# A scheduler's clock for the tensor engine: charging the change between dense and tiled products

## The chip, the core and the metric

The kernel runs on one core of a Trainium2 chip. TensorE (PE) multiplies, VectorE (DVE), ScalarE (ACT) and GpSimd (POOL) work element by element, SyncE (SP) issues DMAs. Each engine takes its own instructions strictly in the order in which they were written, and waits at a semaphore where an operand is not there yet. The metric is the device time of one execution in microseconds (us), median of several runs. Before the change it was 2242.0 us (three runs, 2240.91 to 2247.69).

## The reference

Two transformer blocks over 512 tokens of width 1024, all in float32. The first block (one layer) has three mixers side by side: dilated attention, a gated linear attention (GLA) and block attention. The second block (two layers, with a second stream of 256 context tokens in the first of them) has a Fourier mixer, grouped attention and a gated recurrence (HGRN). Each layer ends in a feed-forward part. The part that matters here is the decay inside GLA and HGRN:

```
# GLA                                           # HGRN, both directions
log_a = log_sigmoid(a_lr @ w_a2 + b_a) / 16     cum   = cumsum(lf, axis=2)
diff  = b[..., :, None, :] - b[..., None, :, :]  diff  = cum[:, :, :, None, :] - cum[:, :, None, :, :]
decay = exp(where(causal, diff, -inf))          decay = exp(where(mask, diff, -inf))
attn  = einsum('ic,jc,ijc->ij', q, k, decay)    att   = einsum('td,sd,tsd->ts', q, k, decay)
```

The rest is matrix products with large weights: `proj = h @ w_in`, `x + mix @ w_out`, `square(relu(h2 @ w_ff1)) @ w_ff2`, `(silu(h @ wg) * (h @ wu)) @ wd`, and the modulation vectors `silu_c @ w_ada`.

## The kernel before, in words

**Dense products.** Every weight tile (128x1024) comes by DMA into a `raw` buffer, is rounded by ACT (`hi`) and its remainder is taken by DVE (`lo`) in the task `split`. A product of a weight block with an activation block then takes three matmuls (hi by hi, hi by lo, lo by hi) into a PSUM tile named `psm` or `psx`. One such triple, 512 or 256 columns wide, is one operation for the scheduler.

**Tiled products.** The decay is not formed pair by pair. GLA and HGRN work in levels of 1, 2, 4, 8 and 16 positions (`LOW`, then 32 and 64). At each level `low_gram` (line 1074) forms small products of 32 columns, placed in different tiles of the PE array, into a PSUM tile named `psd`; DVE copies what the level's mask selects (`copy_predicated`, line 1092). Then `decay_step` or `bidir_level` (lines 1048 and 2046) multiplies K and Q by that level's decay, on DVE or on POOL, whichever the scheduler finds earlier, and `bidir_gram` (line 2061) copies K into order for the next level. So each level of a segment waits for elementwise work of the level before. One `low_gram` is one PE operation of 16 small products (32 in GLA). There are 84 such groups: 14 in GLA (first block), 14 in HGRN over the context, 28 in HGRN of the second block's layer 0 (tasks `hg00`, `hg01`, `hg10`, `hg11`), 28 in layer 1. Below these are stages 1 to 4: a stage runs from the first such group to the last.

**Who sets the order.** The whole kernel is written as Python generators (tasks) that yield operations. `Sched.run` (line 565) keeps a clock for each engine and a finish time for each buffer, asks which pending operation could start earliest by these clocks, writes that one and advances its engine's clock by the operation's `cost`. It runs while the program is built; on the chip only the resulting order of each engine is left. Where an operation may go to several engines (`alt`), the same clocks choose. The table of costs is the planner's, for instance, for a group of tiled products and for a 256-column triple:

```
base = 4 * n / 2.4
if m <= 32:
    return max(32, base / 4 + 14)          # 32 ns each: 512 ns for 16, 1024 ns for 32
...
op.thin = cost < 40 * len(mms)             # in PE(): true for these groups alone
```

A 256-column triple is put down at 333 ns, a 512-column triple at 646 ns. `THIN = (0.7, 500.0, 1.0)` is a second rule for these groups: `s.thin` grows by a group's cost and falls by 0.7 of every other PE cost; above 500 the next group is put back by that much. `s.port` keeps a POOL operation and a DVE operation with two SBUF inputs apart on the planner's clocks.

Of the kernel before, what the change touches and what calls it, by code (L numbers as in the profile page):

```python
# [229 lines left out]
class Fut:  # L230
# [4 lines left out]
    def __init__(s, v=None):  # L235
        s.v, s.ok = v, v is not None
# [199 lines left out]
class Sched:  # L436
# [6 lines left out]
    def __init__(s, tc, pools, counts):  # L443
        s.tc, s.nc = tc, tc.nc
        nc = s.nc
        s.eng = {"pe": nc.tensor, "act": nc.scalar, "dve": nc.vector, "pool": nc.gpsimd, "sp": nc.sync}
        s.clock = {e: 0.0 for e in s.eng}
        s.busy = {e: 0.0 for e in s.eng}
        s.wr, s.rd, s.wre = {}, {}, {}
        s.pools = pools  # L450
        s.freel = {k: list(range(c)) for k, c in counts.items()}
        s.avail = {}
        s.owner = {}
        s.who = {}
        s.tasks = []
        s.n = 0
        s.table = None
        s.thin = 0.0
        s.hold = 0.0
        s.port = {"dve": 0.0, "pool": 0.0}  # L460
        s.low = {k: c for k, c in counts.items()}
        s.marks = []
# [75 lines left out]
    def emit(s, op, st, who=''):  # L538
        e = op.eng
        eng = s.eng[e]  # L540
        if op.table is not None and op.table != s.table:
            eng.preload_act_table_set(SETS[op.table])
        for fn, a, k in op.calls:
            r = getattr(eng, fn)(*a, **k)  # L544
            if s.log is not None:
                s.log.append((r, e, fn, st, op, who))
        cost = op.cost
        if op.table is not None and op.table != s.table:
            cost += 1300
            s.table = op.table  # L550
        end = st + cost
        if e == "pe":
            s.thin = s.thin + cost if op.thin else max(0.0, s.thin - THIN[0] * cost)
        s.clock[e] = end
        if op.port:
            s.port[e] = end
        s.busy[e] += cost
        fin = end + op.lat
        for n in op.outs:
            s.wr[n] = max(s.wr.get(n, 0.0), fin)  # L560
            s.wre[n] = e
        for n in op.ins:
            s.rd[n] = max(s.rd.get(n, 0.0), end if e == "pe" else end + 40)
# [2210 lines left out]
```

## Time and profile before

| | |
|---|---|
| median of 3 runs | 2242.0 us |
| profiled execution | 2240.0 us, of which the span of the trace is 2238.2 us |
| PE busy | 2210.3 us (99% of the span) |
| weight loads of PE | 1924.0 us (86%) |
| DVE busy | 1560.7 us (70%) |
| ACT busy | 916.4 us (41%) |
| POOL busy | 112.7 us (5%) |
| granted TensorE clock | 0.999 of full speed |

A busy PE means that matmul records follow each other without a hole; matmuls overlap, so the length of a record is more than its share of the time. What a product costs is read from the distance between starts. An idle PE is a hole in that chain, and there are 27.9 us of it.

### The profile page before, as it was taken

How to read it: one execution, taken by the hardware profiler on the slowest of the kernel's cores; microseconds unless marked ns; L12 is line 12 of the kernel's file. 1: busy time of each engine (PE TensorE's matmuls, PEld its weight loads, DVE VectorE, ACT ScalarE, POOL GpSimd, SP SyncE). 2: the span in 40 equal slices, each digit the busy share in tenths (PEclk: the TensorE clock that was granted, in tenths of full speed). 3: DMA queues.
4: the chain of work that ended last, by engine and by line, in shares of the span. 5: the costliest groups of instructions: out<-in, count | busy, mean ns of one | idle time of the engine just before them, and what ended most of it. 6: DMA issues, size and time to landing. Idle time of an engine off the chain costs nothing.

```text
span 2238.2 us, 42398 instructions
## 1 busy us (share of the span) xinstructions
PE 2210.3 (99%) x17071; PEld 1924.0 (86%) x17071; DVE 1560.7 (70%) x3754; ACT 916.4 (41%) x1679; POOL 112.7 (5%) x118
## 2 busy tenths in 40 slices
PE   9999999999999999999999999999999999999998
PEld 7887988788888879899888888889979899888887
DVE  6888976888888898798765443557787876444446
ACT  5465644452224455764212112124545754222224
POOL 0100002000000030000000000000040000000000
PEclk9999999999999999999999999999999999999999
DMA  5446443334444621343333212433321223222223
GB/s 197 139 146 189 176 149 125 137 128 146 146 155 166 216 78 48 104 143 138 144 126 128 95 66 78 136 136 119 113 66 58 77 86 123 94 95 102 96 94 113
DMA packets 92116, 272.69 MB, mean 122 GB/s; under 512 B 10944, under 2 KB 20952, under 8 KB 91920
## 3 DMA queue, kind: packets, MB, share of 16 engines
q1 hardware_dynamic: 91920, 269.99, 35.8%
q8 instruction: 134, 2.20, 0.4%
q14 instruction: 62, 0.51, 0.1%
HBM read 253.66 MB, written 7.38 MB: 117 GB/s over the span
## 4 chain that ended last, share of the span: by engine, by line
PE 91%; DVE 4%; DMA 2%; ACT 2%; issue 1%; SPq 0%; DVEq 0%; ACTq 0%
PE psm L544 69%; PE psx L544 18%; PE psd L544 4%; DVE slot L544 3%; DMA rawc<-wada 1%; DVE wu L544 1%; ACT wu L544 1%; ACT slot L544 1%; DMA slot<-ctx 0%; SPq L544 0%; DMA slot<-x 0%; DMA slot<-slot 0%; DMA rawc<-w2in 0%; ACT pr L544 0%; DVE sm L544 0%
## 5 line engine op out<-in xcount | busy, mean ns | idle before, releaser
L544 PE MATMUL psm<-slot,wu 128*128 128x512 f32 (+1 forms) x8406 | 1542.8, 341 | 6.6 <-DVE slot L544 5.0
L544 PEld LDWEIGHTS psm<-slot,wu 128*128 128x128 f32 x8406 | 1305.6, 190 | 188.1 <-DVE slot L544 8.1
L544 ACT CAST wu<-raw 128x1024 fp32r<-128x1024 f32 (+1 forms) x325 | 340.5, 1048 | 860.0 <-PE psm L544 479.1
L544 DVE TENSOR_TENSOR wu<-raw,wu 128x1024 fp32r<-128x1024 f32 (+1 forms) x325 | 402.3, 1238 | 180.8 <-ACT wu L544 175.5
L544 DVE CUSTOM_DVE_ANT_0 slot<-rawc,slot 128x256 f32<-128x256 f32 x640 | 271.4, 424 | 100.7 <-DMA rawc<-wada 90.5
L544 DVE TENSOR_TENSOR slot<-slot,slot 128x256 f32<-128x256 f32 (+5 forms) x362 | 197.0, 554 | 15.2 <-ACT slot L544 12.5
L544 PE MATMUL psm<-wu,slot 128*128 128x256 f32 x1296 | 181.5, 289 | 0.0
L544 DVE SCALAR_TENSOR_TENSOR slot<-psm,mods,slot 128x256 f32<-128x256 f32 (+1 forms) x190 | 108.5, 572 | 104.4 <-PE psm L544 103.2
L544 DVE TENSOR_TENSOR slot<-slot,psm 128x512 f32<-128x512 f32 (+1 forms) x202 | 118.6, 594 | 76.4 <-PE psm L544 71.5
L544 PEld LDWEIGHTS psm<-wu,slot 128*128 128x128 f32 x1296 | 162.7, 191 | 4.0 <-issue 1.2
L544 PE MATMUL psx<-slot,wu 128*128 128x512 f32 (+1 forms) x858 | 164.1, 346 | 0.1
L544 PEld LDWEIGHTS psx<-slot,wu 128*128 128x128 f32 x858 | 137.1, 190 | 19.2 <-DVE wu L544 0.3
L544 PE MATMUL psd<-slot,slot 64*32 64x32 f32 (+6 forms) x3616 | 124.5, 216 | 6.0 <-issue 2.5
L544 PEld LDWEIGHTS psd<-slot,slot 64*32 64x32 f32 (+4 forms) x3616 | 93.5, 116 | 35.7 <-issue 15.8
L544 PE MATMUL psx<-slot,slot 128*64 128x128 f32 (+5 forms) x1554 | 121.3, 281 | 0.9 <-ACT slot L544 0.7
L544 POOL TENSOR_TENSOR slot<-slot,slot 128x256 f32<-128x256 f32 (+1 forms) x72 | 72.6, 1016 | 951.9 <-DVE slot L544 820.1
L544 ACT CAST slot<-slot 128x512 fp32r<-128x512 f32 (+3 forms) x142 | 79.7, 561 | 77.0 <-DVE slot L544 73.9
L544 PEld LDWEIGHTS psx<-slot,slot 128*64 128x64 f32 (+3 forms) x1554 | 91.1, 139 | 23.3 <-issue 10.9
L544 ACT COPY slot<-psx 128x256 f32<-128x256 f32 (+5 forms) x191 | 78.2, 421 | 61.5 <-PE psx L544 53.0
L544 ACT ACTIVATE slot<-slot 128x256 f32<-128x256 f32 (+1 forms) x150 | 65.3, 456 | 33.3 <-DVE slot L544 28.5
L544 ACT ACTIVATE pr<-psd,sm 128x768 f32<-128x768 f32 (+1 forms) x80 | 65.1, 816 | 19.8 <-DVE sm L544 19.1
L544 DVE SCALAR_TENSOR_TENSOR slot<-slot,mods,slot 128x256 fp32r<-128x256 f32 (+2 forms) x152 | 69.0, 492 | 4.6 <-ACT slot L544 4.5
(100 smaller groups left out, 1334.4 us busy)
## 6 DMA issues: line engine op xcount, KB each, us to landing
rawc<-wada SPq DMA_DIRECT2D x96, 512.0 KB, 4.5
raw<-w2gu SPq DMA_DIRECT2D x88, 512.0 KB, 3.3
raw<-w1ff SPq DMA_DIRECT2D x64, 512.0 KB, 3.3
raw<-w2da SPq DMA_DIRECT2D x56, 512.0 KB, 3.2
raw<-w2in SPq DMA_DIRECT2D x36, 512.0 KB, 3.4
raw<-w2out SPq DMA_DIRECT2D x24, 512.0 KB, 3.7
raw<-w1in SPq DMA_DIRECT2D x23, 512.0 KB, 4.0
rawc<-w2in SPq DMA_DIRECT2D x18, 512.0 KB, 3.3
```

What stands on the lines that cost most here:

```text
L544: r = getattr(eng, fn)(*a, **k)
```

## The change

The scheduler remembers whether the last PE operation was a tiled group. When the next one is of the other kind, PE's clock advances by 89 more (dense to tiled) or 210 more (tiled back to anything else). Nothing else is edited: no instruction is added or removed by hand, no buffer and no cost table.

```
@@ -456,6 +456,7 @@
         s.table = None
         s.thin = 0.0
+        s.was_thin = False
         s.hold = 0.0
@@ -548,6 +549,9 @@
         if op.table is not None and op.table != s.table:
             cost += 1300
             s.table = op.table
+        if e == "pe" and op.thin != s.was_thin:
+            cost += 89 if op.thin else 210
+            s.was_thin = op.thin
         end = st + cost
         if e == "pe":
             s.thin = s.thin + cost if op.thin else max(0.0, s.thin - THIN[0] * cost)
```

What comes of it is another order. Both programs have the same 4271 PE operations and the same 84 tiled groups, each of them alone between other work, so 84 changes there and 84 back in either. The first rows below are PE's in stage 4, from one tiled group of a segment on (`psd` is the tiled groups' PSUM tile, `psm` the dense products'; `32x32 x16` is one group, and a row `128x256 x3` one triple). Before:

```order
L544 MATMUL psd_3167_17610<-slot_3161_17533,slot_3166_17608 32x32 x16
L544 MATMUL psm_3169_17614<-wu_3135_17411,slot_2952_16322 128x256 x3
L544 MATMUL psm_3169_17614<-wu_3135_17411,slot_2953_16332 128x256 x3
L544 MATMUL psm_3169_17614<-wu_3135_17411,slot_2955_16343 128x256 x3
L544 MATMUL psd_3178_17649<-slot_3158_17527,slot_3177_17639 32x32 x16
L544 MATMUL psm_3169_17614<-wu_3135_17411,slot_2960_16364 128x256 x3
L544 MATMUL psm_3169_17614<-wu_3135_17411,slot_2952_16322 128x256 x3
L544 MATMUL psm_3169_17614<-wu_3135_17411,slot_2953_16332 128x256 x3
L544 MATMUL psm_3169_17614<-wu_3135_17411,slot_2955_16343 128x256 x3
L544 MATMUL psm_3169_17614<-wu_3135_17411,slot_2960_16364 128x256 x3
L544 MATMUL psm_3169_17614<-wu_3147_17463,slot_2963_16378 128x256 x3
L544 MATMUL psd_3181_17698<-slot_3158_17527,slot_3180_17696 32x32 x16
```

And PE's rows at the same place now, from the same group on:

```order
L545 MATMUL psd_3167_17591<-slot_3161_17533,slot_3166_17589 32x32 x16
L545 MATMUL psm_3146_17462<-slot_3058_16828,wu_3126_17338 128x512
L545 MATMUL psm_3146_17462<-slot_3059_16829,wu_3126_17338 128x512
L545 MATMUL psm_3146_17462<-slot_3058_16828,wu_3126_17338 128x512
L545 MATMUL psd_3168_17616<-slot_3158_17524,slot_3166_17589 32x32 x16
L545 MATMUL psm_3170_17636<-wu_3135_17411,slot_2952_16322 128x256 x3
L545 MATMUL psd_3174_17645<-slot_3161_17533,slot_3173_17643 32x32 x16
L545 MATMUL psm_3170_17636<-wu_3135_17411,slot_2953_16332 128x256 x3
L545 MATMUL psd_3181_17672<-slot_3172_17638,slot_3173_17643 32x32 x16
```

Three triples and then six stood between the groups; now it is one each time, and the triples that stood here come later. Over whole stages, rows of PE's order from the first tiled group to the last: 151 and 114 (stage 1), 144 and 110, 165 and 145, 155 and 100 (stage 4).

The second place is POOL in stage 4, the multiplies of K (`slot_3087`, `slot_3088`) and Q (`slot_3158`) by the decay of the segments `hg00` and `hg01`. Before:

```order
L544 TENSOR_TENSOR slot_3087_17034<-slot_3087_17034,slot_3159_17529 128x32x2x4
L544 TENSOR_TENSOR slot_3087_17034<-slot_3087_17034,slot_3159_17529 128x16x2x8
L544 TENSOR_TENSOR slot_3158_17527<-slot_3158_17527,slot_3159_17529 128x16x2x8
L544 TENSOR_TENSOR slot_3087_17034<-slot_3087_17034,slot_3159_17529 128x8x2x16
L544 TENSOR_TENSOR slot_3088_17035<-slot_3088_17035,slot_3162_17538 128x16x2x8
L544 TENSOR_TENSOR slot_3088_17035<-slot_3088_17035,slot_3162_17538 128x8x2x16
```

And now, from the same multiply on:

```order
L545 TENSOR_TENSOR slot_3087_17034<-slot_3087_17034,slot_3159_17526 128x32x2x4
L545 TENSOR_TENSOR slot_3088_17035<-slot_3088_17035,slot_3162_17535 128x32x2x4
L545 TENSOR_TENSOR slot_3087_17034<-slot_3087_17034,slot_3159_17526 128x16x2x8
L545 TENSOR_TENSOR slot_3088_17035<-slot_3088_17035,slot_3162_17535 128x16x2x8
L545 TENSOR_TENSOR slot_3087_17034<-slot_3087_17034,slot_3159_17526 128x8x2x16
L545 TENSOR_TENSOR slot_3158_17524<-slot_3158_17524,slot_3159_17526 128x8x2x16
L545 TENSOR_TENSOR slot_3098_17109<-slot_3098_17109,slot_3096_17107 128x128x2
L545 TENSOR_TENSOR slot_3184_17720<-slot_3184_17720,slot_3096_17107 128x128x2
L545 TENSOR_TENSOR slot_3087_17034<-slot_3087_17034,slot_3159_17526 128x4x2x32
L545 TENSOR_TENSOR slot_3158_17524<-slot_3158_17524,slot_3159_17526 128x4x2x32
```

More of the multiplies have gone to POOL here: 28 within stage 4, where there were 21. On DVE, operations between the masked copy of a stage's first group and that of its last are 84 before and 72 now in stage 1, 85 and 81 in stage 2, 124 and 127 in stage 3, 121 and 105 in stage 4. POOL's are 11 and 8, 15 and 12, 20 and 21, 21 and 28.

The dense triples within the stages, counted the same way on PE: 256 columns wide 31 and 20, 24 and 24, 55 and 46, 58 and 32; 512 columns wide 16 and 16, 33 and 23, 6 and 6, 6 and 6. Of other small PE operations (transposes, 64-column products, attention) 8, 2, 2 and 3 fewer stand within the stages now.

## Rows read from the trace of the kernel before

**Rows 1.** The page: span, and busy us by engine.
```profile
span 2238.2 us, 42398 instructions
PE 2210.3 (99%) x17071; PEld 1924.0 (86%) x17071; DVE 1560.7 (70%) x3754; ACT 916.4 (41%) x1679; POOL 112.7 (5%) x118
```

**Rows 2.** Stretches: stages 1 to 4, then two of attention; length, then busy us.
```profile
core 0: us, PE busy (x) PEld busy (x) DVE busy (x) ACT busy (x) POOL busy (x), PEclk, DMA share, GB/s
39.75:79.95 40.20, 38.89 (x1008) 32.24 (x1011) 34.40 (x120) 13.80 (x32) 6.29 (x9) 1.00 0.43 130
364.70:406.70 42.00, 41.30 (x657) 32.04 (x662) 39.69 (x95) 19.06 (x33) 16.54 (x15) 1.00 0.33 108
787.50:832.60 45.10, 43.16 (x1160) 35.63 (x1161) 44.15 (x128) 22.75 (x57) 18.95 (x20) 1.00 0.23 66
1633.00:1680.00 47.00, 44.07 (x1186) 36.63 (x1183) 42.54 (x122) 21.42 (x56) 20.77 (x21) 1.00 0.18 57
850.00:900.00 50.00, 49.85 (x428) 44.81 (x427) 42.79 (x90) 32.98 (x78) 2.96 (x2) 1.00 0.14 43
1700.00:1750.00 50.00, 50.00 (x426) 45.75 (x425) 40.28 (x82) 30.64 (x75) 5.65 (x4) 1.00 0.14 43
```

**Rows 3.** Timeline of PE in dense stretches: start us, length us, operation, count.
```profile
1030.75 3.04 PE L544 MATMUL psx<-slot,wu 128*128 128x256 f32 x24
1033.63 5.92 PE L544 MATMUL psm<-slot,wu 128*128 128x256 f32 x48
...
1206.18 5.63 PE L544 MATMUL psx<-slot,wu 128*128 128x512 f32 x24
1211.65 0.62 PE L544 MATMUL psm<-slot,wu 128*128 128x512 f32 x2
```

**Rows 4.** Timeline near the end of stage 4 (a group of 16 shows as x32).
```profile
1669.90 0.41 DVE L544 TENSOR_TENSOR slot<-slot,slot 128x256 f32<-128x256 f32 x1
1669.92 0.89 POOL L544 TENSOR_TENSOR slot<-slot,slot 128x256 f32<-128x256 f32 x1 [0.53 <-ACT slot L544]
...
1669.93 0.35 PE L544 MATMUL psd<-slot,slot 64*32 64x32 f32 x32
...
1670.22 0.97 PE L544 MATMUL psx<-wu,slot 128*128 128x256 f32 x6
1670.23 0.66 DVE L544 TENSOR_TENSOR slot<-slot 128x64 f32<-128x64 f32 x1
1670.82 0.29 DVE L544 COPY_PREDICATED slot<-c_masks,psd 128x128 f32<-128x128 int32 x1
...
1671.11 0.35 PE L544 MATMUL psd<-slot,slot 64*32 64x32 f32 x32
```

**Rows 5.** Timeline in the middle of stage 4, up to a wait of PE.
```profile
1654.46 1.93 POOL L544 TENSOR_TENSOR slot<-slot,slot 128x256 f32<-128x256 f32 x2 [5.34 <-DVE slot L544]
...
1655.32 1.22 DVE L544 COPY slot<-slot 128x64 f32<-128x64 f32 x2
...
1657.51 0.79 PE L544 MATMUL psd<-slot,slot 64*64 64x64 f32 x48 [1.12 <-DVE slot L544]
...
1660.35 0.60 PE L544 MATMUL psx<-c_ident,slot 128*128 128x128 f32 x4
```

**Rows 6.** Groups on POOL by form: count, busy us, mean ns, idle before.
```profile
L544 POOL TENSOR_TENSOR slot<-slot,slot 128x256 f32<-128x256 f32 x63 | 59.9, 961 | 803.1 <-DVE slot L544 718.8 <-PE psd L544 77.3 <-DVE part L544 5.7
L544 POOL TENSOR_TENSOR slot<-slot,sm 128x256 f32<-128x256 f32 x3 | 1.8, 611 | 0.8 <-DVE sm L544 0.8
```

**Rows 7.** Who PE waited for over the whole span: us, times, longest.
```profile
PE psm L544 <- DVE slot L544: 5.0, 12, 1.4
PE psx L544 <- DVE slot L544: 4.9, 7, 1.8
...
PE psd L544 <- DVE slot L544: 2.1, 4, 1.1
```

More of the change, by code (lines that the diff above doesn't have):

```diff
@@ L458, in __init__ @@
         s.thin = 0.0
+        s.was_thin = False
         s.hold = 0.0
@@ L550, in emit @@
             s.table = op.table
+        if e == "pe" and op.thin != s.was_thin:
+            cost += 89 if op.thin else 210
+            s.was_thin = op.thin
         end = st + cost
```

## The prediction

> **What bounds the kernel now.** I read the page first: PE is busy for 2210.3 of 2238.2 us and no other engine for more than 70% [rows 1]. So the time is PE's work plus 27.9 us of holes, and no order can take away the work. Then I looked at who ends PE's holes: it is mostly DVE (5.0, 4.9 and 2.1 us for its three kinds of PSUM tile) [rows 7]. The share of 70% is a mean over unlike stretches, so the third view was the busy time by stretch, cut at the four stages in which the tiled groups stand. There DVE is busy for 34.40 of 40.20, 39.69 of 42.00, 44.15 of 45.10 and 42.54 of 47.00 us, PE for 38.89, 41.30, 43.16 and 44.07 [rows 2]. In stage 3 DVE has less room left (0.95 us) than PE (1.94 us). These 174.30 us are the place where the change acts, and in them two engines run side by side at nearly full load. PE's idle time there is 1.31 + 0.70 + 1.94 + 2.93 = 6.9 us.
>
> **What is charged, and what it takes.** A row of 24 products of 256 columns starts at 1030.75 and the next row at 1033.63, so one product has 0.120 us and a triple 0.36; with 512 columns it is (1211.65 - 1206.18) / 24 = 0.228, a triple 0.684 [rows 3]. The planner has 0.333 and 0.646: too little. Now a tiled group: it starts at 1669.93, the dense row behind it at 1670.22, and the next group at 1671.11 [rows 4]. The group itself takes 0.29, and the six dense products have 0.89 where 0.72 would do, so the change there and back costs 0.17. Group and both changes take 0.46 us. The planner had put down 0.512 for the group alone, which covered them already; now it puts down 0.512 + 0.089 + 0.210 = 0.81. It was 0.05 us too dear and is 0.35 us too dear. (In GLA's groups of 32 the base is 1.024.)
>
> [...]
>
> **The change part by part.** No instruction goes or comes, so PE's work as a whole stays: 0 us. The number of changes stays: 0 us. What moves is which dense triples stand within the stages. While elementwise work readies the next tiled group, the planner fills PE; each group now uses up 0.3 us more of that wait on PE's clock, so fewer triples fit. The second rule on these groups is not what moves them: before, one 256-column triple brought its account from 512 to 279, below the 500 at which it acts; now from 601 to 221.
>
> Between the first and the last group of each stage there is less PE work, then, while the elementwise work of 84 levels is still all there. I price both sides for each stage. A 256-column triple counts 0.36, a 512-column one 0.684, one of the small operations 0.6 (four transposes had 0.60 [rows 5]). DVE's demand I take as its busy time, scaled by the operations in its order, since records and waits for POOL are all in that time.
>
> Stage 1: 11 triples of 0.36 and 8 small operations leave, 4.0 + 4.8; PE has 38.89 - 8.8 = 30.1. DVE: 34.40 x 72/84 = 29.5. PE still sets the pace, its idle time stays: 0.
>
> Stage 2: 10 triples of 0.684 and 2 small, 6.8 + 1.2; PE has 33.3. DVE: 39.69 x 81/85 = 37.8. PE idles 4.5 instead of 0.7: +3.8.
>
> Stage 3: 9 triples of 0.36 and 2 small, 3.2 + 1.2; PE has 38.8. DVE: 44.15 x 127/124 = 45.2. PE idles 6.4 instead of 1.9: +4.5.
>
> Stage 4: 26 triples of 0.36 and 3 small, 9.4 + 1.8; PE has 32.9. DVE: 42.54 x 105/121 = 36.9. But seven more multiplies go to POOL, at least 0.61 each by the shortest group of that size [rows 6], 4.3 in all, and I add them to DVE's: 41.2. PE idles 8.3 instead of 2.9: +5.4.
>
> Why add POOL's time to DVE's? The 128x256 multiplies of this kind have a mean of 961 ns, and others of that size 611 [rows 6]. In rows 4 one starts at 1669.92, beside a DVE multiply that runs until 1670.31, and lasts 0.89; DVE's next, a small multiply of 128x64, starts at 1670.23 and lasts 0.66, until just after POOL's end at 1670.81. They take turns. In rows 5 two POOL multiplies run to 1656.39, DVE's two tiny copies from 1655.32 take 1.22, and PE ends a wait of 1.12 us for DVE at 1657.51: this is what a hole in a stage looks like, and I expect more of them.
>
> [...]
>
> The triples that leave are done elsewhere, where PE has no holes for them: two stretches of attention show 49.85 and 50.00 of 50.00 busy [rows 2]. So the new holes are lost.
>
> Sum: 3.8 + 4.5 + 5.4 = 13.7 us. The profiled execution took 2240.0 us (span 2238.2 and 1.8 around it), which gives 2253.7, about 2254. The median of the runs, 2242.0, is 2.0 above that execution; from it the sum would give 2256.
>
> **Bounds.** Below: DVE's busy time holds waits for POOL and the tails of records that overlap the next one, and if all that gives way, DVE fits under PE in each stage and nothing is lost: 2240. The idle time there now could even go: 2233. Above: if the stages took as long as before (each level's chain as slow as now), all the PE work moved out would become holes, 8.8 + 8.0 + 4.4 + 11.2 = 32.4: 2272. I take 13.7, because stage 3 shows an engine that could hardly do its work faster than it did, and the others are then in the same state.
>
> **The rivals.**
>
> A, no change. The planner allows for more latency than the chip needs, and DVE packs its work more tightly when it is waited for; the stages shrink by about what left them. For it: DVE has 4 to 6 us of room in stages 1 and 4 [rows 2]. Against it: 0.95 us in stage 3, with more operations after than before. About 2241.
>
> B, faster. A later PE clock has the planner put a tiled group behind its operands' real arrival, not ahead of it; PE's holes in the stages close (6.9 us), to 2233. It decides if those holes were groups placed too early and DVE has room to come in time. For it: dense triples are still priced below what they take (0.333 against 0.36), and the surcharge makes up for that on PE's clock. Against it: there are fewer triples, not more, between a group and the next, which gives DVE less time, not more. A fall in the number of changes would do it too, but there is none.
>
> C, the whole 32 us. The chains of levels, not DVE's throughput, set the stage lengths: 2265 to 2272. For it: each level waits for the one before. Against it: near the end of stage 4 two segments alternate with 1.18 us from group to group [rows 4], far quicker than a stage's mean of 1.7 (47.00 / 28), so chains can run faster than they do.
>
> **How the numbers follow.** Forecast (a loss in stages 2 to 4, 2247 to 2265 as its own range) 0.58; A 0.22; B 0.12; C 0.08. Under 0.3% (6.7 us) a change can't be told from none here. Faster 0.12, the same 0.22, slower 0.58 + 0.08 = 0.66. The range leaves out most of B and the end of C: 2238 to 2270.
>
> **What would show it.** PE's busy time stays within a few us of 2210 and its idle time grows from 27.9 to some 42, ended by DVE, at `psd` and at the dense products behind it. The stages, cut at their first and last group, become shorter, to about 31, 38, 45 and 41 us, with PE below 90% in 3 and 4 and DVE above 95% in 3. The attention stretches stay at full PE. It is wrong if the stages come out near 31, 34, 41 and 36 with PE still full (A), if PE's idle time in the stages is below 6.9 us (B), or if holes outside the stages carry the difference.

## The result, and the profile after

The changed kernel takes 2266.1 us (median of 4 runs, 2261.6 to 2267.2) where before, now with four runs, takes 2241.5: a ratio of 1.0107, 95% interval 1.0094 to 1.0119. It is slower by 24.7 us. The forecast was 2254, slower by 13.7: the sign was right, and nearly half of the size was missing. Two executions further down, one of e10 and the profiled one of e12, ran at a mean granted clock of 0.75 and took some 450 us longer; they are left out of the ratios.

The profiled execution took 2267.2 us. First its page, busy us by engine, to be set beside [rows 1]:

```profile
span 2265.4 us, 42392 instructions
PE 2222.0 (98%) x17071; PEld 1931.6 (85%) x17071; DVE 1553.7 (69%) x3729; ACT 922.2 (41%) x1694; POOL 130.6 (6%) x128
```

PE has the same 17071 products. The span is 27.2 us longer, and that splits in two: PE stands idle for 43.4 us (2265.4 - 2222.0) instead of 27.9, which is +15.5, and it is busy for 11.7 us more with the same work. The two profiles lie at opposite ends: after's is the slowest of its four runs, with the lowest mean clock (0.993, the others 0.994 and 0.995), and before's, with 2240.0 us, is faster than any of its four. So these 27.2 us, and the clock's share of them above all, are on the high side. The stages, cut at their first and last tiled group as in [rows 2], with the same columns (length, then busy us; the last three are granted clock, DMA share, GB/s):

```profile
core 0: us, PE busy (x) PEld busy (x) DVE busy (x) ACT busy (x) POOL busy (x), PEclk, DMA share, GB/s
40.43:78.72 38.29, 34.30 (x954) 27.78 (x954) 30.90 (x98) 9.61 (x19) 4.54 (x7) 0.91 0.42 132
374.27:410.25 35.98, 33.73 (x628) 25.79 (x629) 35.48 (x87) 17.75 (x35) 14.66 (x12) 1.00 0.33 107
801.35:848.58 47.23, 39.60 (x1142) 32.02 (x1142) 47.06 (x136) 21.24 (x55) 21.32 (x21) 0.96 0.22 70
1653.26:1696.17 42.91, 36.66 (x1084) 28.42 (x1083) 37.56 (x102) 16.85 (x43) 27.59 (x29) 0.88 0.13 39
```

Length less PE's busy time gives the holes: 3.99, 2.25, 7.63 and 6.25, in all 20.1 us where before had 6.9. That is +13.2 of the +15.5. The first waits of PE over the whole span (us, times, longest) say who ends them, to be set beside [rows 7]:

```profile
PE psd L545 <- DVE slot L545: 13.0, 18, 1.9
PE psx L545 <- DVE slot L545: 5.0, 7, 3.1
PE psm L545 <- DVE slot L545: 4.5, 10, 1.4
PE psm L545 <- issue: 3.8, 2, 2.2
```

Tiled groups (`psd`) that wait for DVE went from 2.1 to 13.0 us; the dense products' waits for DVE are as before. ("issue" is a hole in which PE waits for nothing that the profile shows; more on these at the end.) The other half of the loss stands in the third column from the end: the granted clock is 0.91, 0.96 and 0.88 in stages 1, 3 and 4, where [rows 2] have 1.00. Here are three of the falls, each with the stretch ahead of it (length, PE busy, granted clock, DMA share, GB/s):

```profile
core 0: us, PE busy (x), PEclk, DMA share, GB/s
45.00:51.30 6.30, 4.13 (x139) 1.00 0.72 242
51.30:58.10 6.80, 6.78 (x140) 0.50 0.03 12
820.00:829.50 9.50, 6.51 (x234) 1.00 0.04 10
829.50:833.00 3.50, 3.50 (x77) 0.51 0.34 132
1677.00:1686.30 9.30, 7.20 (x281) 1.00 0.01 4
1686.30:1699.90 13.60, 13.38 (x249) 0.50 0.05 11
```

Half clock here is a granted clock of 0.50 or 0.51, as in the second row of each pair. Each of these falls comes behind a stretch in which PE was busy for 66 to 77% of the time. The reverse does not hold: between 1658.7 and 1666.7 us, in the same profile, PE is busy for 5.67 of 8.00 us (71%), and the clock stays full (1.00) for another 19 us, up to 1686.3. With a fourth of 3.41 us at 133.23, PE ran 27.3 us at half clock. In the profile of before there is no such stretch until the program's last microseconds (0.77 between 2230 and 2238.2). So each profile can be split: span = PE's work at full clock + holes + half of the time at half clock, which is 13.65 us for after. After: 2208.4 + 43.4 + 13.65 = 2265.4; before: 2210.3 + 27.9 + 0. The half is the author's estimate, and rather high: six products of 256 columns and the tiled group behind them take 1.19 us at full clock (1666.99 to 1668.18) and 1.97 in the last stretch (1692.15 to 1694.12), so 0.40 of the time is lost there, which for 27.3 us would be 10.9 and for the work 2211.1. The work is what is left over in this sum; that it comes out near 2210 each time, by either figure, is what speaks for the split.

The last hole of note lies outside the stages, in the attention behind stage 1. A stretch of it with all engines (as in the stages above), and then from the timeline the DMA, the DVE operation and the PE operation in question:

```profile
130.00:133.00 3.00, 0.60 (x3) 0.16 (x1) 0.00 (x1) 1.03 (x1) 0.00 (x0) 1.00 1.02 247
```

```profile
127.39 1.61 SPq L545 DMA_DIRECT2D slot<-relg  x2
133.00 0.42 DVE L545 CUSTOM_DVE_ANT_0 slot<-rawc,slot 128x256 f32<-128x256 f32 x1 [4.29 <-DMA slot<-relg]
133.69 0.47 PE L545 MATMUL psx<-c_ident,slot 128*128 128x128 f32 x1 [3.09 <-DVE slot L545]
```

DVE stands for 4.29 us at a product for the modulation vectors (`rawc` is a tile of `w_ada`) that still waits for a transfer, with the DMA engines full (1.02). Which transfer is open: the product waits for two semaphores, and the profile names the gather `relg` here, but `rawc` itself at the same place in e6 below. The small operation whose result PE's transpose needs is queued behind it on DVE, so PE stands for 3.09 us, and the clock falls behind that hole too. In before the corresponding gather (`relg`) was issued at 120.67, and DVE's wait for `rawc` there was 0.88 us.

### The profile page after: what moved, and what is told of

Read it like the earlier page. It is cut to its first block, busy times and chain, and to the rows that moved or that the text cites. A ratio compares the mean times of both kernels' runs of the same rounds, so it can differ in the third digit from the quotient of the medians.

```text
span 2265.4 us, 42392 instructions
## 1 busy us (share of the span) xinstructions
PE 2222.0 (98%) x17071; PEld 1931.6 (85%) x17071; DVE 1553.7 (69%) x3729; ACT 922.2 (41%) x1694; POOL 130.6 (6%) x128
## 4 chain that ended last, share of the span: by engine, by line
PE 89%; DVE 6%; issue 1%; DMA 1%; ACT 1%; SPq 0%; POOL 0%; DVEq 0%; ACTq 0%
PE psm L545 67%; PE psx L545 19%; DVE slot L545 4%; PE psd L545 4%; DVE wu L545 1%; DMA rawc<-wada 1%; ACT wu L545 1%; SPq L545 0%; ACT slot L545 0%; DMA slot<-x 0%; DMA slot<-ctx 0%; DMA rawc<-w2in 0%; DVE at L545 0%; ACT at L545 0%; DVE pr L545 0%
## 5 line engine op out<-in xcount | busy, mean ns | idle before, releaser
L545 PEld LDWEIGHTS psm<-slot,wu 128*128 128x128 f32 x8286 | 1289.6, 190 | 187.5 <-issue 9.6
L545 DVE TENSOR_TENSOR slot<-slot,slot 128x256 f32<-128x256 f32 (+4 forms) x360 | 199.0, 561 | 20.1 <-ACT slot L545 15.0
L545 PE MATMUL psx<-slot,wu 128*128 128x512 f32 (+1 forms) x978 | 186.9, 345 | 0.3 <-DVE wu L545 0.3
L545 PEld LDWEIGHTS psx<-slot,wu 128*128 128x128 f32 x978 | 155.4, 190 | 21.6 <-DVE wu L545 0.5
L545 PEld LDWEIGHTS psx<-slot,slot 128*64 128x64 f32 (+3 forms) x1554 | 91.2, 139 | 24.5 <-issue 11.7
L545 ACT COPY slot<-psx 128x256 f32<-128x256 f32 (+5 forms) x204 | 82.9, 418 | 67.3 <-PE psx L545 59.5
L545 DVE TENSOR_REDUCE sm<-psd 128x1 f32<-128x768 f32 (+1 forms) x80 | 66.3, 843 | 14.8 <-PE psd L545 14.5
L545 DVE TENSOR_TENSOR slot<-psx,slot 128x128 fp32r<-128x128 f32 (+7 forms) x153 | 50.7, 347 | 35.7 <-ACT slot L545 33.5
```

## The experiments

The theory T: the surcharge takes dense work out of the stages, so tiled groups are reached before the elementwise work for them is done (holes), and behind stretches with holes the clock is lower. Rivals: L, the order of before is a lucky one and any other costs some microseconds; C, the chain of levels sets the stage lengths, not DVE's load; and, for the clock, that the tiled products themselves bring it down.

All ratios are against before on the same chip, where its medians were 2245.4 us beside e1 to e8 and 2244.3 beside e9 to e12. The expectations start from 2242, so a time in them is to be read with 2 to 3 us added. "Half clock" leaves out the program's end, "work" is PE busy less half of the half-clock time; both, and the holes, are of the one profiled execution.

| kernel | time, us | ratio [95%] | holes | half clock | work |
|---|---|---|---|---|---|
| before | 2241.5 | 1 | 27.9 | 0 | 2210.3 |
| after | 2266.1 | 1.0107 [1.0094, 1.0119] | 43.4 | 27.3 | 2208.4 |
| e1, stages 1 and 2 | 2264.5 | 1.0076 [1.0049, 1.0104] | 42.3 | 23.9 | 2210.8 |
| e2, stage 3 | 2255.3 | 1.0039 [1.0026, 1.0052] | 37.3 | 17.1 | 2209.0 |
| e3, stage 4 | 2249.1 | 1.0013 [0.9999, 1.0027] | 31.2 | 13.7 | 2209.7 |
| e4, sign reversed | 2251.7 | 1.0028 [1.0014, 1.0041] | 34.1 | 13.7 | 2209.7 |
| e5, 1 and 2 ns | 2244.5 | 0.9998 [0.9987, 1.0008] | 29.1 | 3.4 | 2211.0 |
| e6, stage 1 | 2250.2 | 1.0026 [1.0016, 1.0036] | 34.0 | 17.1 | 2209.2 |
| e7, holes filled | 2264.6 | 1.0086 [1.0072, 1.0100] | 31.1 | 6.8 | 2229.0 |
| e8, less DVE work | 2259.1 | 1.0058 [1.0045, 1.0072] | 41.0 | 13.7 | 2210.1 |
| e9, no POOL | 2267.5 | 1.0105 [1.0091, 1.0119] | 45.2 | 13.7 | 2213.4 |
| e10, before, no POOL | 2242.1 | 0.9996 [0.9986, 1.0005] | 28.3 | 0 | 2211.5 |
| e11, half surcharge | 2258.4 | 1.0064 [1.0050, 1.0078] | 43.0 | 3.4 | 2211.5 |
| e12, reversed in 3, 4 | 2245.4 | 1.0004 [0.9995, 1.0013] | - | - | - |

The work column stays within 2208 and 2214 but for e7, which adds some. So, to within some 5 us, the orders differ in holes and clock alone.

**Which stage costs what (e1, e2, e3, e6).** The condition was put on PE's planned time:

```
-        if e == "pe" and op.thin != s.was_thin:
+        if e == "pe" and s.clock["pe"] < 6e5 and op.thin != s.was_thin:            # e1
+        if e == "pe" and 6e5 < s.clock["pe"] < 1.2e6 and op.thin != s.was_thin:    # e2
+        if e == "pe" and 1.2e6 < s.clock["pe"] and op.thin != s.was_thin:          # e3
+        if e == "pe" and s.clock["pe"] < 2e5 and op.thin != s.was_thin:            # e6
```

> The surcharge counts only in the first two stages (GLA and the context's HGRN); the order of stages 3 and 4 is then that of before. Theory (DVE-bound holes inside the stages, and a TensorE clock that falls behind them): the losses belong to their stages and add up. From the trace of after: holes +2.7 and +1.6 us, 6.8 us at half clock in stage 1 (3.4 lost), and, if the order of the attention behind stage 1 comes along, a hole of 2.9 and 3.4 us at half clock (1.7). 2250 to 2254. Rival (a reshuffle anywhere in the program happens to be worse, the stages are not special): no such split, anything from 2240 to 2266, and the three parts e1 to e3 do not add up to 24.7.

> The surcharge counts only in stage 3. Theory: holes there from 1.9 to some 7 us, one short stretch at half clock, 2242 + 5.5 + 1.7 = 2249. Its PE work between first and last group is even 1.5 us less than in after, so a little more is possible (2251). Rival (reshuffle): no relation to what stage 3 lost in after.

> The surcharge counts only in stage 4, whose order is then exactly that of after. Theory: holes +3.3 us, and 13.7 us at half clock behind them (6.8 lost): 2252. If the clock keeps its full level with the same holes, 2245. Rival (reshuffle): no relation; 2242 or below is possible.

> The surcharge in stage 1 alone; the orders behind it follow. In e1, stage 1 itself had no new holes (4.4 us idle) but PE waited 3 us near 133 us behind a late transfer and ran at half clock for 17 us around both places. Theory T2 (stage 1's shorter length moves the attention behind it ahead of its transfers; a hole there, and two falls of the clock): 2250 to 2257, with the hole at 126 to 137 us again. Rival (e1's loss comes from stage 2 or from the places behind it): 2241 to 2247.

The three excesses add up to 1.28%, and after has 1.07%: roughly additive in time, and stages 1 and 2 carry most, not stages 3 and 4 as forecast. In place they do not add up: e1 has 14.4 us of holes more than before, of which 4.9 lie within the stages, and after has 15.5, of which 13.2 do. So part of e1's loss is its own, and the sum of the three is partly chance. e1 cost more than expected, e2 somewhat more, e3 less; e3's interval reaches down to no loss at all. e3's stage 4 had after's holes (5.9 us), but 6.8 us at half clock, where after's profile has 13.65. e6 is as expected in place: PE's longest wait behind stage 1 is at the transfer again, 2.0 us before 134 (us, times, longest). In time its loss is less than expected, 5.8 us by the ratio where 8 to 15 were:

```profile
PE psx L545 <- DVE slot L545: 2.0, 1, 2.0
```

The difference between e1 and e6, some 11 us by the ratios, belongs to the surcharge in stage 2, although the holes within stage 2 grew by 1.5 us only. In e1's profile PE waits behind it, between 420 and 950 us, so (e6 has 0.4 and 2.0 us of these two kinds there):

```profile
PE psx L545 <- DVE slot L545: 4.0, 2, 3.8
PE psm L545 <- DVE slot L545: 2.0, 2, 1.4
```

The 3.8 us end at 943.9, behind stage 3; there DVE comes to the two operations that PE needs behind six others. The order of the other engines behind a stage follows from the planner's clocks within it, and that can be paid far away. Why it comes out worse just there was not settled, and these waits are only a part of the 11 us.

**Is it any other order, or this one? (e5, e11)**

```
-            cost += 89 if op.thin else 210
+            cost += 1 if op.thin else 2        # e5
+            cost += 45 if op.thin else 105     # e11
```

> The change with a surcharge of 1 and 2 ns in place of 89 and 210. The order is shuffled in small ways over the whole program, but the PE work that the plan puts between the first and the last group of each stage stays (35.0, 36.3, 38.2, 37.0 us by trace prices, where before has 35.0, 37.6, 35.7, 37.0 and after 28.7, 29.4, 31.5, 26.0). Theory T (thinner stages make the holes, and the holes make the clock fall): as before, 2241 to 2248. Rival L (before's order is a lucky one, and any other order costs some us wherever a queue comes out worse): 2250 to 2262.

> The change with half the surcharge (45 and 105 ns). The plan puts 37.0, 34.8, 37.8 and 36.0 us of PE work into stages 1 to 4 by trace prices, changes of tiling counted; before has 37.7, 40.3, 41.0, 42.3 and after 31.4, 32.1, 36.8, 31.3. Theory T (the loss goes with the PE work taken out of the stages): stage 1 as before, the others between; with 17 of after's 30 us of work taken out, 2250 to 2259. Rival (loss only where stage 1 is thinned and the attention behind it comes ahead of its transfers): 2242 to 2247.

e5 costs nothing: rival L, that any other order costs something, falls for the part that e5 changes. That is not the whole program. By tiles and shapes the first 3755 products of PE in e5 are those of before, to 400.5 us there, and DVE's first difference is at 392.6 us; so stage 1 and the attention behind it are not tried. e11 gives stage 1 nearly before's work by the plan, and it still has 3.3 us of holes there instead of 1.31, most of them "issue" holes: for stage 1, L stays open. Half the surcharge costs about 60% of the whole: the loss grows with the surcharge. e11's profile has after's holes with hardly any half clock, and its four times lie within 0.6 us of each other although their mean clocks go from 0.995 to 0.998. So holes and half clock are likely not independent: the author's reading is that a slow clock costs nothing where PE would have waited anyway, which no run shows by itself (the holes of the other three runs were not seen). The split above says where the time went, not what it would be without one of its terms.

**What brings the clock down (e7).** One more dense product ahead of each group, into the group's own PSUM tile (`s.ones` is a tile of ones; the lines that hand it over are left out here):

```
+        if op.thin:
+            t = s.owner[op.calls[0][1][0].tensor.name][2]
+            eng.matmul(t[:, :P], s.ones, s.ones, start=True, stop=True, skip_group_check=True)
```

> The kernel after with one more product of 128 columns (all ones, overwritten by the group) ahead of each of the 84 tiled groups; no other order. It takes 0.2 to 0.4 us by the row of such products at the start of the program, 18 to 35 us in all, and some of it fills holes. Theory T (the falls of the clock follow stretches in which PE stands idle for a good part): PE's idle time in the stages falls from 20 us to under 10 and no half clock in stages 3 and 4; the time 2262 to 2285, less than the added work. Rival (the tiled products or the changes themselves bring the clock down): half clock in stages 1, 3 and 4 as in after, 20 us and more in all.

The rival for the clock falls. Tiled groups, changes of tiling and order are after's; the holes went from 43.4 to 31.1 us and the half clock from 27.3 to 6.8. The mean clocks of its four runs, 0.997 and 0.998, lie above all of after's. Not quite as expected, stage 3 keeps one fall of 3.4 us. Stages 3 and 4 (length, PE busy, clock, DMA share, GB/s):

```profile
799.00:848.80 49.80, 46.18 (x1198) 0.97 0.22 67
1654.10:1695.70 41.60, 39.77 (x1139) 1.00 0.15 40
```

The 84 products are 20.6 us of added work by the table (0.245 each), and the time did not rise at all. Of these, 12.3 us went into holes and by the split 10.25 us came back from the clock (8.2 by the 0.40 above). So in after's order the holes cost their length and, by way of the clock, up to nearly as much again, and the useless work put into them was free. But what a hole costs in clock is not fixed. These are the stretches around stages 3 and 4 in e9 (below), which has after's order on PE (columns as in the stages above):

```profile
799.00:848.00 49.00, 43.14 (x1106) 35.95 (x1094) 46.65 (x169) 22.82 (x59) 0.00 (x0) 0.90 0.21 63
1650.00:1696.00 46.00, 39.33 (x1135) 30.36 (x1134) 43.21 (x143) 21.34 (x53) 0.00 (x0) 1.00 0.17 49
```

The second has more holes than the first, 6.67 us against 5.86, and no fall of the clock. e11's 43.0 us of holes went with 3.4 us at half clock. What decides between the two was not found.

**What sets the holes in the stages (e8, e9, e10).** e8 takes DVE work away that is on no chain of levels; e9 and e10 issue POOL's multiplies to DVE, in the order of after and of before:

```
+            if fn == "tensor_tensor_reduce" and a[1].tensor.name.startswith("rawc"):     # e8
+                a = tuple(x[:, :16] for x in a[:3]) + tuple(a[3:])
-        eng = s.eng[e]                                                                   # e9, e10
+        eng = s.eng["dve" if e == "pool" and op.calls[0][0] == "tensor_tensor" else e]
```

> The kernel after, with the products and sums that build the modulation vectors on DVE (operand rawc) done over 16 of their 256 columns: part of the computation is left out, the order is after's. That frees some 0.3 us each, 4 to 8 us of DVE per stage where 10 to 24 of them stand (8.7 us busy in stage 3), none of it on the chain of levels. Theory T (DVE's throughput sets the holes): stage 3 idle from 7.6 to under 4 and stage 4 likewise lower, stages shorter, fewer falls of the clock: 2245 to 2257. Rival C (the chain of levels sets the lengths): holes within 1.5 us of after's, 2261 to 2267.

> The kernel after, with every multiply that the plan gave to POOL issued to DVE instead, at the same place in the order. In stage 3 that puts 21 multiplies more on DVE, 0.41 us each where DVE works alone (8.6 us), and takes 21.3 us of POOL's records away. Theory P (POOL and DVE take turns, so a multiply on POOL costs DVE as much as it takes on POOL): DVE's busy time in stage 3 stays within 3 us of 47.1 although it has 21 operations more, the time within 2260 to 2269. Rival (the two work side by side): stage 3 longer by some 6 us, stages 2 and 4 too, the time 2272 to 2285.

> The same edit in the kernel before: POOL's multiplies issued to DVE. Theory P (turns): 2237 to 2246, holes in the stages about as before (6.9 us), or fewer. Rival (side by side): stage 3 has 0.95 us of room on DVE and gets 20 x 0.41 = 8.2 us more, stage 2 gets 6.1 and has 2.3: 2250 to 2260.

e8 falls between its two expectations: by its loss against before, 13 us, it is where the theory put it, by its holes nearer to the rival. DVE lost 151 us of work over the span, the time fell by some 0.5%, and the holes by 2.4 us only (stage 3 has 5.9, stage 4 6.2). But their kind changed. Its first waits of PE:

```profile
PE psd L547 <- DVE slot L547: 8.0, 14, 1.8
PE psd L547 <- issue: 5.7, 5, 1.9
PE psm L547 <- DVE slot L547: 4.8, 11, 1.4
```

The groups' waits for DVE went from 13.0 to 8.0 us, so DVE's load did set a good part of them; 8.0 remain, where before has 2.1. The chain of levels is the likely reason for these. In after's stage 4, PE's groups wait 4.0 us for DVE, and DVE stands for 4.6 us waiting for PE's groups, which is what a chain that goes to and fro between the two looks like; no run takes the chain away. In the place of the rest came holes that "issue" ends, in which PE waits for nothing that the profile shows: 8.8 us in all with those at `psm`, where after has 4.8.

e9 and e10 settle the price of a multiply on POOL. In e9's page the work of POOL is gone:

```profile
PE 2220.2 (98%) x17071; PEld 1926.6 (85%) x17071; DVE 1572.7 (69%) x3851; ACT 922.9 (41%) x1694; POOL 2.0 (0%) x6
```

DVE does 122 operations more in 19.0 us more, which is 0.16 each, though such a multiply takes 0.41 alone; and the time is after's. The reason stands in DVE's groups in stage 3 (count, busy us, mean ns of one), first after and then e9:

```profile
L545 DVE TENSOR_TENSOR slot<-slot,slot 128x256 f32<-128x256 f32 x32 | 16.0, 525 | 0.0
L545 DVE CUSTOM_DVE_ANT_0 slot<-rawc,slot 128x256 f32<-128x256 f32 x15 | 8.7, 582 | 0.1
```

```profile
L545 DVE TENSOR_TENSOR slot<-slot,slot 128x256 f32<-128x256 f32 x55 | 22.1, 445 | 0.0
L545 DVE CUSTOM_DVE_ANT_0 slot<-rawc,slot 128x256 f32<-128x256 f32 x15 | 6.3, 418 | 0.1
```

Without POOL beside them these operations have 445 and 418 ns instead of 525 and 582 (the first group now with the 23 moved into it): DVE's records had held the turns of POOL. Stage 4 says it too: between 1650 and 1696 us DVE is busy for 43.21 us in e9 and for 39.39 in after, 3.8 more, although 28.57 us of POOL's work there are gone. e10 says the same of before: 2242.1, a ratio of 0.9996, with all but 2.0 of POOL's 112.7 us moved to DVE. Had the two worked side by side, both would by the rivals' estimates have been slower by 6 us and more.

**The other sign (e4, e12).**

```
-            cost += 89 if op.thin else 210
+            cost = max(10.0, cost - (89 if op.thin else 210))     # e4; e12 only where s.clock["pe"] > 6e5
```

> The sign is turned: 89 and 210 are taken off PE's clock at the same places. More dense triples stand in the stages then (PE work between first and last group some 39, 37, 54 and 49 us by the prices of the trace, against 38, 40, 41 and 42 before), while DVE's is 28, 29, 41 and 38. Theory: DVE has room in stages 3 and 4, holes there shrink from 4.9 to 1 to 3 us, the clock stays full: 2235 to 2242. Rival (the planner's order of before is tuned to its own clock, any shift of it loses): 2250 or more.

> The sign of the surcharge turned round, as in e4, but in stages 3 and 4 alone: 53.6 and 49.4 us of PE work within them where before has 41.0 and 42.3; stages 1 and 2 as before. Theory T: holes in stages 3 and 4 from 4.8 us to under 1.5, no fall of the clock there, nothing new ahead of them: 2236 to 2241, faster than before. Rival (longer stages cost elsewhere, as e4's other holes may say): 2243 to 2252.

Both miss: no version beats before. e4 did fill stages 3 and 4, as the second of these stretches shows (columns as in the stages above), but stage 1, the first, got holes and half clock:

```profile
40.00:90.00 50.00, 44.90 (x1027) 37.44 (x1025) 33.24 (x108) 14.13 (x32) 7.10 (x11) 0.90 0.36 110
800.00:856.00 56.00, 55.98 (x1239) 50.08 (x1235) 50.13 (x145) 27.61 (x67) 19.43 (x23) 1.00 0.28 85
```

And dense work drawn into stage 3 is missing behind it. Between 850 and 1050 us PE is busy for 98.68 and 95.59 of 100, where before has 99.58 and 100.00: 5.3 us of new holes. And between 130 and 133 us PE stands as it does in after, busy for 0.30 of 3.00. e12 kept stages 1 and 2 as before and came out with no change; its profile can't be compared with the others, so that the place behind stage 3 took its gain back is only inferred from e4.

## Why the prediction was right in sign and short in size

**What leaves the stages: right.** PE's work within them, at full clock, was put at 30.1, 33.3, 38.8 and 32.9 us. The rows give 34.30 - 3.4 = 30.9 (6.8 us of stage 1 were at half clock), 33.7, 39.60 - 1.7 = 37.9 and 36.66 - 4.9 = 31.7.

**Holes in the stages: right in sum, not in place.** 13.7 was forecast, 13.2 came. By stage it was 0, 3.8, 4.5, 5.4, and came 2.7, 1.6, 5.7, 3.3: misses of +2.7, -2.2, +1.2 and -2.1 that cancel, so the close sum is luck. The step that failed is "PE still sets the pace, its idle time stays" in stage 1 and DVE's scaled busy time in 2 and 4, which was put at 37.8 and 41.2 us and came to 35.48 and 37.56. In stages 2 and 3 DVE is the limit, as forecast, with 35.48 of 35.98 and 47.06 of 47.23 us. In stage 1 it is busy for 30.90 of 38.29, so its load can't be the limit; the two holes of 2.19 and 1.63 us there are "issue" holes (below). Nor can it be in stage 4, with 37.56 of 42.91: the 6.25 us of holes there were forecast from a load that did not come.

**POOL added to DVE: right in kind, not in size.** By e9 and e10 the two take turns: with 128.6 us of POOL's work issued to DVE in e9, DVE is busy for 19.0 us more. But the 4.3 us that the forecast put on top of DVE's scaled 36.9 in stage 4 did not come: DVE's record has 37.56.

**Moved triples are lost work time: right.** No stretch of PE's work disappears; the work column says so.

**PE busy within a few us of 2210: wrong, and this is the missing term.** It came to 2222.0. The forecast had holes cost their own length; here they also cost the clock behind them, 13.65 us in this profile by the split (10.9 by the 0.40 above). By the split, the profiled execution's 27.2 us are 13.2 of holes in the stages, 2.3 of holes elsewhere and 13.65 of the clock, less 2.0 by which PE's work came out smaller. In [rows 2] the clock is 1.00 everywhere, with PE busy for 94% and more of each stage; the stretches ahead of after's falls have 66 to 77%, and the forecast itself put PE at 80 to 88% of the length of stages 2 to 4 and did not ask what the clock would do there.

**Holes elsewhere:** said to count against the forecast, and there are some, 2.3 us net in after, with the 3.09 at 130.6 to 133.7.

**The rivals.** A fails: the holes grew, and DVE packed its work hardly tighter anywhere (0.35 us an operation in stage 3 before and after). B fails: groups that the planner put later on PE's clock waited more, not less; and e4, with the opposite sign, gained nothing either. The time itself, 2266.1, lies 1 us above the forecast's own range (2247 to 2265) and in C's (2265 to 2272), but C's way was another: it wanted 32 us of holes, and there are 15.5 and the clock. Its chains may be what is seen in e8, in the 8.0 us of waits that stay when DVE is relieved.

## What to carry to other kernels

In a planner, the price of an operation is also a decision on how much other work stands beside it: ask what the price will draw away or in, before asking whether it is the true price. Where TensorE is the bound, as here, price a hole for its length, put up to as much again into the range for the clock behind it (e7: 12.3 us of holes, and 8.2 to 10.25 of clock), and look for stretches in which several holes come close together (three of the falls here came behind stretches in which PE was busy for 66 to 77%). An engine's busy time near 100% can hold its waits for another engine (in stage 3 DVE was busy for 47.06 of 47.23 us with multiplies of 525 ns, and they took 445 in e9, with POOL's work gone), so relieve it in an experiment before you take it for load.

## What the runs showed of the hardware that was not expected

Useless products put into holes cost nothing here, and less of the profile is at half clock: +20.6 us of work, 2264.6 us where after has 2266.1, half clock 6.8 us instead of 27.3 (e7).

The mean clock of an execution is not fixed by the program: runs of one kernel have mean clocks from 0.994 to 0.998 (e2), and in e2 the time goes with them, from 2258.8 us down to 2253.8. Before has such runs too: beside e1 its runs went from 2241.4 us at a mean clock of 0.999 to 2254.0 at 0.996.

PE has holes that no other engine ends, in the middle of a group or a triple. In after one such hole is this:

```profile
51.32 1.01 PE L545 MATMUL psm<-slot,wu 128*128 128x512 f32 x2 [2.19 <-issue]
```

It comes behind the 476th product of the program, and in e8, with the same order, a hole of 0.45 us stands behind the same 476th; both have one behind the 986th too (1.63 and 2.65). What PE stands for there, the profile does not say. In after a packet of 16 KB of the DMA queue that the trace calls "instruction" ran from 47.90 to 50.06 us, into the hole that ends at 51.32, with the DMA engines busy for 0.94 of that time; 70 of the 134 such packets took less than 1.0 us. At the 986th product the nearest packet took 1.37 us, from 69.96 to 71.32, and the hole ends at 72.88. Whether the holes have to do with these packets was not shown; no experiment tried it.
